# A two-layer trunk kernel on one core: T4 made in B21's buffer, and the two layer norms of the first ffn's end set beside other products

## The chip, the cores and the metric

The kernel runs on one core of one Trainium2 chip. Its time is device microseconds of one execution; the figure for a kernel is the median of several runs. The profile is of one further execution.

## The reference

Two streams of 256 tokens and width 1024, a context and a latent one, pass through two layers. Layer 0 mixes with a bidirectional mLSTM, layer 1 with latent attention (MLA), in which the latent queries see the keys and values of both streams. After each mixer comes a gated convolutional ffn, and after each sublayer a layer norm over the residual. Only the latent stream is returned. Cut to what matters here:

```
x = layer_norm(ALPHA * x + gate * mixer(h))           # both streams
f = (silu(dwconv(gate_part)) * up_part) @ ffn_w_out   # 2816 -> 1024
x = layer_norm(ALPHA * x + gate5 * f)                 # both streams
# layer 1, MLA: h = x * (1 + scale) + shift
kc, vc = kv(h_ctx)        # h @ w_dkv -> rms norm -> @ w_ukv
kl, vl = kv(h_lat)        # the same, with rotary keys
ql = rms_norm(h_lat @ w_dq) @ w_uq
y = attend(ql, [kc, kl], [vc, vl]) @ w_out
```

## The kernel before

Everything is float32. Each product runs as three float32r matmuls on halves "hi" and "lo" of both operands (`mm3`, L383 to L385): hi.hi, hi.lo, lo.hi. The halves are made by `split`: ScalarE copies (L388, for weights L323), VectorE subtracts (L389, L326).

**Weights** come through one stream in a fixed order (`_plan`). A tile of 128x1024 is loaded by the SP queue into a raw buffer (`_load`), split into one of three `w` buffers (or, when marked wide, into two buffers of the large pool `u`), used, and released. `use` splits ahead up to eight tiles, but no more than three `w` tiles live at once. The raw buffers form a ring; a tile takes the ring's next place.

**Value product and ffn output** (`w_v`, L787, and `w_fout0`, L1365) use a seven-product scheme of Strassen's kind over 2x2 blocks: four products on sums of weight blocks (vt2, v11, vt3, vt1; yt2, y11, yt3, yt1), then products with B21 (v21, y21), with T4 (vt4, yt4) and with B22 (v22, y22). T4 is T2 + B21 as the signs are set here: the sum T2 is formed by VectorE in the raw buffer (`_sum`, L292 to L294), written to DRAM as `t2d` when it is split (L325), and for T4 read back by SP (L278), after which POOL adds the block B21 from the weights with an adding load (L279). There are 14 such tiles, eight in `w_v` and six in `w_fout0`. In `w_v` the three last products alternate tile by tile; in `w_fout0` they run y21 (six tiles), y22 (six), yt4 (six, of which the last three by halves of the tokens).

**Around the ffn's end.** After the first four products of `w_fout0`, eight PSUM banks are held (p6, p1, p7, p5, two each). ScalarE copies p1 (u1, L1434), VectorE makes u2, u3, v and u4 from the others (L1437 to L1446). `residual` multiplies each by its gate (L1454) and adds ALPHA times the residual x1 (L1455), loaded by POOL from `x1d`. `add` (L1460) brings in the last products: gate, sum, statistics (L1464 to L1466). `z_norm` (L1502) normalises rows, `ln_T` (L1191) transposes them on TensorE and makes the modulated halves hc (context) and hl (latent) by L1206 to L1212; `ln_x` (L1217) writes the normed rows to DRAM for the next residual. Operands of y21, y22 and yt4 come back from DRAM and are converted (`operand`, L1386 and L1387).

**Order of the MLA part.** y22 ends the context's rows; the context's norm, its transposes and its dkv product come amid the yt4 tiles (`mid`, `mla_ctx`), then ukn(0), uv(0), uv(1) of the context run while the latent rows get their last product, norm and transposes in the background generator (`tick` takes one step of it); then in `mla` (L1633) the latent dkv and dq products, ukn(1), the query products and uv of the latent. Engine orders are the framework's scheduler's, except inside `manual_schedule`, where the program's order is kept, and for single pinned instructions. Limits on the stream (`st.limit`, PA, PB, PC with `pump`) time the splits of the wide tiles. `ffn_in` (L1292) of layer 1 runs its first pair of tiles with three matmuls per k and later pairs with two, one of them 512 columns wide (L1320), followed by a copy and an add.

Of the kernel before, what the change touches and what calls it, by code (L numbers as in the profile page):

```python
# [25 lines left out]
H1 = 8  # L26
# [11 lines left out]
PA, PB, PC = 0, 2, 4  # L38
# [18 lines left out]
YTAIL = 3  # L57
# [13 lines left out]
def _plan():  # L71
# [12 lines left out]
    for p in range(2):  # L84

        for j in range(4):
            for n in ("vt2", "v11", "vt3", "vt1"):
                add((n, p, j), 1024)
        for j in range(4):
            for n in ("v21", "vt4", "v22"):  # L90
                add((n, p, j), 1024)
# [15 lines left out]
    for n in ("y21", "y22", "yt4"):  # L107
        for j in range(6):
            if (n, j) == ("yt4", 6 - YTAIL):
                for c, m in enumerate((3, 3, 2)):  # L110
                    add(("dkv", 0, c), m * 320)
            add((n, 0, j), cols[j], n == "yt4" and j >= 6 - YTAIL)
# [4 lines left out]
    for c in range(4):  # L117
        add(("dq", 0, c), 768)
# [14 lines left out]
def _pack(i):  # L133
# [12 lines left out]
    for key, (n, cols) in ids.items():  # L146
        kind, a, c = key
        if kind == "up":
# [5 lines left out]
        elif kind[0] in "vy":  # L154

            x, y = {"11": (0, 0), "t1": (0, 1), "21": (1, 0), "t4": (1, 0)}.get(kind[1:], (1, 1))
# [78 lines left out]
class Stream:  # L235
# [26 lines left out]
    def _room(self):  # L262

        if self.nl >= self.n:
            return False
        j0, ring = self.ring(self.nl)
        tag = ring[(self.nl - j0) % len(ring)][0]
        return [self.tags[j] for j in self.raw].count(tag) < [x[0] for x in ring].count(tag)

    def _load(self):  # L270
# [3 lines left out]
        j0, ring = self.ring(j)  # L274
        tag, bufs = ring[(j - j0) % len(ring)]
        t = k.pool.tile([128, CW], F32, tag=tag, name="raw", bufs=bufs)
        if key[0] in ("vt4", "yt4"):
            k.nc.sync.dma_start(t[:, :cols], k.t2d[key[0][0], key[1], key[2]][:, :cols])  # L278
            k.nc.gpsimd.dma_start(t[:, :cols], self.ws[n, :, :cols], accum_op=ALU.add)  # L279
        elif key[0] not in ("vt2", "yt2"):  # L280
            k.nc.sync.dma_start(t[:, :cols], self.ws[n, :, :cols])
# [14 lines left out]
    def _split(self):  # L296
# [25 lines left out]
        else:  # L322
# [3 lines left out]
            k.nc.vector.tensor_sub(l[:, :cols], src, h[:, :cols])  # L326
        self.hl[j] = (h, l)
# [27 lines left out]
class K:  # L355
# [431 lines left out]
    def w_v(self):  # L787
# [16 lines left out]
        for p in range(2):  # L804
# [26 lines left out]
            p2, p4, p3 = pair("tok"), pair("tok"), pair("tok")  # L831
            for i in range(4):
                for name, ps, x in (("v21", p2, 2), ("vt4", p4, 3), ("v22", p3, "S4")):
                    w = st.use((name, p, i))
                    for h in range(2):
                        prod(ps, A[x, 2 * i + h], w, h, 2 * i + h)
                    self.tick(1)
                    if p == 1 and len(self.xc) < 16:
                        self.xc_load(len(self.xc) + len(self.xcr))
# [377 lines left out]
    def ln_x(self, ln, zs, dst):  # L1217
# [74 lines left out]
    def ffn_in(self, l, hT, n, nt, pre=(), both=None):  # L1292
# [6 lines left out]
        for p in range(NF):  # L1299
            pss = []  # L1300
            for j in range(2):
# [5 lines left out]
                else:  # L1307
# [13 lines left out]
                    if both is not None and p > 0:  # L1321
# [43 lines left out]
    def w_fout0(self, x1d, mid):  # L1365
# [4 lines left out]
        parts = [("2", i) for i in range(6)] + [("S4", i) for i in range(6)] + [("3", i) for i in range(6)]  # L1370
# [34 lines left out]
        n = 0  # L1405
        for i in range(6):
            for name, ps, x in (("yt2", p6, "S2"), ("y11", p1, "1"), ("yt3", p7, "S3"), ("yt1", p5, "S1")):
# [7 lines left out]
                if n >= 8:  # L1415
                    operand()
# [6 lines left out]
                if n >= 16 and n % 2 == 0:  # L1423
                    if n == 16:
                        z = []
                    t = self.uf("z")
                    nc.gpsimd.dma_start(t, x1d[len(z)])
                    z.append(t)
                n += 1
        stats = [self.tiny(12, "st").rearrange("p (a b) -> p a b", b=6) for _ in range(4)]  # L1430
        u1, u3, u4, vv = [], [], [], []
        for b in range(2):
            u = self.s2("u1")
            nc.scalar.copy(u, p1[b])  # L1434
            u1.append(u)
            u = self.s2("u2")
            nc.vector.tensor_tensor(u, p6[b], u1[b], op=ALU.add)  # L1437
            u4.append(u)
        for b in range(2):
            u = self.s2("u3")  # L1440
            nc.vector.tensor_tensor(u, p7[b], u4[b], op=ALU.add)
            u3.append(u)
        for b in range(2):
            v = self.s2("v")
            nc.vector.tensor_tensor(v, p5[b], u3[b], op=ALU.subtract)
            nc.vector.tensor_tensor(u4[b], p5[b], u4[b], op=ALU.subtract)  # L1446
            vv.append(v)

        def residual():

            for us, g, c in ((u1, 0, lo), (u4, 0, hi), (u3, 1, lo), (vv, 1, hi)):
                for b in range(2):
                    zz = z[2 * g + b]
                    nc.vector.tensor_tensor(us[b], us[b], gate[g][:, c], op=ALU.mult)  # L1454
                    nc.vector.scalar_tensor_tensor(zz[:, c], zz[:, c], ALPHA, us[b], op0=ALU.mult, op1=ALU.add)  # L1455
                    if us is vv:
                        nc.vector.bn_stats(stats[2 * g + b][:, 1], zz[:, c])
# [526 lines left out]
```

## Time and profile before

| what | value |
|---|---|
| median of 3 runs | 1385.51 us (1384.81 to 1386.47) |
| the profiled execution | 1386.22 us |
| its span in the trace | 1384.1 us |
| TensorE (PE) busy | 1354.0 us, 98% |
| VectorE (DVE) busy | 1090.0 us, 79% |
| ScalarE (ACT) busy | 713.1 us, 52% |
| DMA | 297.58 MB, mean 215 GB/s |

In the rows, PE is TensorE, DVE VectorE, ACT ScalarE, POOL GpSimd, SP the queue that loads weights. A row of the view in order of time reads: start, length, engine, source line, operation, output<-inputs, shape, count, and in brackets the idle time before it and what ended that. A row of the waits reads: engine and line that waited, engine and line that ended the wait, total us, times, longest. Matmul lengths overlap; the distance from start to start is what a matmul costs.

### The profile page before, as it was taken

Reading aid. Unit: us, or ns where it says so; the run is one execution under the profiler, and the core shown is the slowest. Engines: PE = TensorE matmul, PEld = TensorE weight load, DVE = VectorE, ACT = ScalarE, POOL = GpSimd, SP = SyncE. Lnnn points to the kernel's source line nnn. Section 1 sums busy time; section 2 is a strip of 40 time slices with the busy share of each in tenths; the row PEclk is TensorE's granted clock in tenths of the full one; section 3 lists DMA queues with packets and bytes.
Section 4 is the critical chain, followed back from the end, with each engine's and each line's share of the span. In section 5 each row is a group of like instructions: output and inputs, shape, how many; then the busy total and the mean of one; then the engine's idle time right before and its main releaser. Section 6 shows DMA issues by size and latency. Waiting matters only on the chain.

```text
span 1384.1 us, 18592 instructions
## 1 busy us (share of the span) xinstructions
PE 1354.0 (98%) x6567; PEld 1123.2 (81%) x6567; DVE 1090.0 (79%) x1768; ACT 713.1 (52%) x1221; POOL 121.6 (9%) x215
## 2 busy tenths in 40 slices
PE   7999999999999999999999999999999999999997
PEld 3788888888788888878898888888777888888886
DVE  6598857687688697779799878668898789788873
ACT  6585534435444555364643434334637567466660
POOL 0033000011011011120002000000001001000100
PEclk9999999999999999999999999999999999999999
DMA  9689847789666364766747877646987425256750
GB/s 338 227 293 316 290 156 247 239 286 302 214 200 204 105 232 132 250 193 228 241 147 239 300 230 234 212 145 229 312 231 226 137 99 202 109 185 185 252 202 31
DMA packets 97900, 297.58 MB, mean 215 GB/s; under 512 B 12136, under 2 KB 24808, under 8 KB 97808
## 3 DMA queue, kind: packets, MB, share of 16 engines
q1 hardware_dynamic: 68672, 218.52, 47.5%
q0 software_dynamic: 17472, 57.57, 13.3%
q10 hardware_dynamic: 11664, 20.32, 4.1%
q8 instruction: 51, 0.84, 0.2%
q14 instruction: 41, 0.34, 0.1%
HBM read 262.90 MB, written 33.46 MB: 214 GB/s over the span
## 4 chain that ended last, share of the span: by engine, by line
PE 91%; DVE 5%; ACT 2%; issue 1%; DMA 0%; SPq 0%; DVEq 0%; ACTq 0%
PE fin L1320 9%; PE fin L383 6%; PE fin L384 6%; PE fin L385 6%; PE tok L383 6%; PE tok L384 6%; PE tok L385 6%; PE y L384 5%; PE y L385 5%; PE y L383 5%; PE qk L383 4%; PE qk L385 4%; PE qk L384 4%; PE up L383 2%; PE up L385 2%; PE up L384 2%
## 5 line engine op out<-in xcount | busy, mean ns | idle before, releaser
L326 DVE TENSOR_TENSOR w<-raw,w 128x1024 fp32r<-128x1024 f32 (+3 forms) x290 | 348.1, 1203 | 141.3 <-ACT w L323 140.3
L323 ACT CAST w<-raw 128x1024 fp32r<-128x1024 f32 (+3 forms) x290 | 300.4, 1037 | 306.2 <-PE tok L385 88.6
L512 DVE SCALAR_TENSOR_TENSOR junk<-ar,bc 128x1024 f32<-128x1024 f32 x128 | 156.0, 1218 | 4.9 <-ACT bc L554 2.1
L384 PE MATMUL fin<-h,w 128*128 128x512 f32 (+1 forms) x376 | 141.2, 376 | 0.0
L385 PE MATMUL fin<-h,w 128*128 128x512 f32 (+1 forms) x376 | 140.9, 375 | 0.0
L383 PE MATMUL fin<-h,w 128*128 128x512 f32 (+1 forms) x376 | 140.8, 376 | 0.1
L1320 PE MATMUL fin<-h,w 128*128 128x256 f32 (+1 forms) x640 | 113.0, 339 | 0.0
L1320 PEld LDWEIGHTS fin<-h,w 128*128 128x128 f32 x640 | 98.2, 189 | 14.7
L383 PE MATMUL qk<-xc,w 128*128 128x512 f32 x256 | 100.7, 393 | 0.0
L385 PE MATMUL qk<-xc,w 128*128 128x512 f32 x256 | 99.9, 390 | 0.0
L384 PE MATMUL qk<-xc,w 128*128 128x512 f32 x256 | 99.8, 390 | 0.0
L384 PEld LDWEIGHTS fin<-h,w 128*128 128x128 f32 x376 | 70.8, 188 | 12.9 <-DVE h L1212 0.2
L385 PEld LDWEIGHTS fin<-h,w 128*128 128x128 f32 x376 | 70.8, 188 | 12.9
L383 PEld LDWEIGHTS fin<-h,w 128*128 128x128 f32 x376 | 70.5, 188 | 13.1 <-ACT h L1211 0.3
L383 PEld LDWEIGHTS qk<-xc,w 128*128 128x128 f32 x256 | 48.1, 188 | 10.0 <-issue 0.4
L385 PEld LDWEIGHTS qk<-xc,w 128*128 128x128 f32 x256 | 48.1, 188 | 9.9
L384 PEld LDWEIGHTS qk<-xc,w 128*128 128x128 f32 x256 | 48.1, 188 | 9.7
L383 PE MATMUL up<-hT,w 128*128 128x512 f32 x128 | 50.5, 394 | 0.5 <-ACT hT L388 0.5
L384 PE MATMUL up<-hT,w 128*128 128x512 f32 x128 | 50.1, 392 | 0.5 <-DVE hT L389 0.5
L385 PE MATMUL up<-hT,w 128*128 128x512 f32 x128 | 50.1, 391 | 0.3 <-DVE w L389 0.3
L383 PE MATMUL tok<-w,hT 128*128 128x512 f32 x128 | 49.8, 389 | 0.0
L384 PE MATMUL tok<-w,hT 128*128 128x512 f32 x128 | 49.8, 389 | 0.0
(463 smaller groups left out, 3151.2 us busy)
## 6 DMA issues: line engine op xcount, KB each, us to landing
raw<-in_ws SPq DMA_DIRECT2D x287, 512.0 KB, 4.3
ar<-in_adaT SPq DMA_DIRECT2D x80, 512.0 KB, 4.6
adaw<-in_ada_w SPq DMA_DIRECT2D x32, 256.0 KB, 6.7
t2d<-raw ACTq DMA_DIRECT2D x13, 512.0 KB, 4.9
raw<-t2d SPq DMA_DIRECT2D x13, 512.0 KB, 6.3
raw<-in_ws POOLq DMA_DIRECT2D x13, 512.0 KB, 8.0
zr<-fd ACTq DMA_DIRECT2D x33, 128.0 KB, 3.9
xmd<-xr POOLq DMA_DIRECT2D x16, 256.0 KB, 5.0
```

The source lines that it names most:

```text
L323: k.nc.scalar.copy(h[:, :cols], src)
L326: k.nc.vector.tensor_sub(l[:, :cols], src, h[:, :cols])
L383: mm(out, w[0], x[0], start=start, stop=False)
L384: mm(out, w[0], x[1], start=False, stop=False)
L385: mm(out, w[1], x[0], start=False, stop=stop)
L512: nc.vector.scalar_tensor_tensor(o, w, 1.0, self.bc[j], op0=ALU.mult, op1=ALU.mult, accum_out=col[:, k, j:j + 1])
L1320: nc.tensor.matmul(o, a, b, start=k == 0 and i == 0, stop=k == 7 and i == 1)
```

## The change

T4 is no longer loaded. When v21 or y21 has been split, POOL adds `t2d` into the raw buffer that still holds B21, and that buffer is T4's raw tile; a buffer is therefore held longer, and `_load` takes any free place of the ring in place of the next one. The orders of the products follow two written lists, V_ORDER and Y_ORDER. In `w_fout0` y21 and yt4 now alternate with PE and DVE in program order, and y22 comes last. u1 is copied as soon as p1 is complete. The residual is added by POOL's adding loads of `x1d`, which `ln_x` of layer 0 writes already multiplied by ALPHA. yt4's end completes the latent rows: their norm and transposes run in the background beside y22 (PE in program order). The context's rows are completed by y22: their norm is emitted before the latent dkv, their transposes after the latent dq. In `mla` the latent keys and values come first, then the context's dkv, and the rest. The pumps go; dkv tiles are wide.

```
+V_ORDER = [("v21", 0), ("v22", 0), ("v21", 1), ("v22", 1), ("vt4", 0), ("v21", 2), ("v22", 2), ("vt4", 1),
+           ("v21", 3), ("v22", 3), ("vt4", 2), ("vt4", 3)]
+Y_ORDER = [("y21", 0), ("y21", 1), ("y21", 2), ("y21", 3), ("yt4", 0), ("y21", 4), ("yt4", 1), ("y21", 5),
+           ("yt4", 2), ("yt4", 3), ("yt4", 4), ("yt4", 5)]
...
 in _plan, after the first four products of the ffn output
+    for n, j in Y_ORDER:
+        add((n, 0, j), cols[j])
+    for j in range(6):
+        add(("y22", 0, j), cols[j])
+    for c, m in enumerate((3, 3, 2)):
+        add(("dkv", 0, c), m * 320, True)
+    for c in range(4):
+        add(("dq", 0, c), 768)
...
 in _load
-            k.nc.sync.dma_start(t[:, :cols], k.t2d[key[0][0], key[1], key[2]][:, :cols])
-            k.nc.gpsimd.dma_start(t[:, :cols], self.ws[n, :, :cols], accum_op=ALU.add)
...
 in _split, after the subtraction
+        if key[0] in ("v21", "y21"):
+            i = [x[0] for x in self.order].index((key[0][0] + "t4",) + key[1:])
+            k.nc.gpsimd.dma_start(src, k.t2d[key[0][0], key[1], key[2]][:, :cols], accum_op=ALU.add)
+            self.raw[i], self.tags[i] = raw, self.tags[j]
...
 in ln_x, scale = ALPHA for layer 0's first norm
-                nc.vector.tensor_tensor(zs[t][:, c], zs[t][:, c], g[h], op=ALU.mult)
-                nc.vector.tensor_tensor(zs[t][:, c], zs[t][:, c], b[h], op=ALU.add)
+                nc.vector.scalar_tensor_tensor(zs[t][:, c], zs[t][:, c], scale, g[h], op0=ALU.mult, op1=ALU.mult)
+                nc.vector.scalar_tensor_tensor(zs[t][:, c], b[h], scale, zs[t][:, c], op0=ALU.mult, op1=ALU.add)
...
 in ffn_in
-                        if both is None or p == 0:
+                        if both is None or p < 2:
...
 in w_fout0
-                if n >= 8:
+                if n >= 6:
                     operand()
...
+                if (name, i) == ("y11", 5):
+                    for b in range(2):
+                        u = self.s2("u1")
+                        pin(nc.scalar.copy(u, p1[b]))
+                        u1.append(u)
...
+        z = [self.uf("z") for _ in range(4)]
+        def sums():
+            def part(us, g, c):
                 for b in range(2):
+                    zz = z[2 * g + b][:, c]
+                    nc.vector.tensor_tensor(zz, us[b], gate[g][:, c], op=ALU.mult)
+                    nc.gpsimd.dma_start(zz, x1d[2 * g + b][:, c], accum_op=ALU.add)
...
+        with self.tc.manual_schedule(engines={e.PE, e.DVE}):
+            self.bg.append(sums())
+            for n, (name, i) in enumerate(Y_ORDER):
+                ps, x = pr[name]
+                if not ps:
+                    ps += pair()
+                w = st.use((name, 0, i))
+                prod(ps, x, w, i)
+                if n == 8:
+                    self.drain()
+                    self.bg.append(add(0, lo, pr["y21"][0]))
+                self.tick(1)
+                operand()
+                if n == 11:
+                    for b in range(2):
+                        nc.vector.bn_stats(stats[2 + b][:, 1], z[2 + b][:, hi])
         self.drain()
+        self.bg = [add(1, lo, pr["yt4"][0]), self.z_norm(z[2:4], stats[2:4]), latent(z[2:4])]
+        with self.tc.manual_schedule(engines={e.PE}):
+            ps = pair()
+            for i in range(6):
+                w = st.use(("y22", 0, i))
+                prod(ps, "S4", w, i)
+                self.tick(2)
+            self.drain()
+        for _ in add(0, hi, ps):
+            pass
+        for _ in self.z_norm(z[0:2], stats[0:2]):
+            pass
+        return z[0:2]
...
 in ukn, per pair of heads
+            if h % 2:
+                for i in range(2):
+                    u = self.kn[h - 1 + i]
+                    self.split(u[:, 0, cs], u[:, 1, cs], ps[:, i * 256:(i + 1) * 256])
...
 mla(hl, hc, ctx): the order of its products
+        self.rope_load()
...
+        wd = [st.use(("dkv", 0, c)) for c in range(3)]
+        rows2 = self.dkv_rows(self.dkv_mm(hl, wd), 2)
         pss = [self.ps("dq0"), self.ps("dq1")]
...
+        self.dkv_T(rows2, 2)
+        ctx()
+        rows = self.dkv_rows(self.dkv_mm(hc, wd), 0)
+        self.take_late()
+        self.tick()
...
+        self.ukn(1)
+        self.tick()
+        self.uv((2, 3))
+        self.dkv_T(rows, 0)
         cq = []
...
+        self.ukn(0)
+        self.tick()
...
+        self.uv((0, 1))
...
 in build
+        def latent(zs):
+            cols = k.ln_mod_cols(1, 1, 0, 0)
+            hlu.extend([k.u("hl") for _ in range(4)])
+            yield from k.ln_T(zs, *cols, hl, True)
+            k.late.append(k.ln_x(1, zs, [x2d[0], x2d[1]]))
+        def ctx():
+            hcu.extend([k.u("hc") for _ in range(4)])
+            for _ in k.ln_T(zc, *k.ln_mod_cols(1, 1, 0, 1), hc, False):
+                pass
+        st.limit = [x[0] for x in order].index(("aout", 0, 0))
+        zc = k.w_fout0(x1d, latent)
+        att = k.mla(hl, hc, ctx)
```

More of the change, by code (lines that the diff above doesn't have):

```diff
@@ L88, in _plan @@
                 add((n, p, j), 1024)
-        for j in range(4):
-            for n in ("v21", "vt4", "v22"):
-                add((n, p, j), 1024)
+        for n, j in V_ORDER:
+            add((n, p, j), 1024)
     add(("gates", 0, 0), 256)
@@ L1439, in w_fout0 @@
[L1439 to L1451, printed above, removed]
-                for b in range(2):
[L1453 to L1457, printed above, removed]
-                    yield
+                n += 1
```

210 lines of the change are left out of this document (73 added, 137 removed).

## The prediction

> **What bounds the kernel now.** I read the page, then what TensorE waited for in the stretch that the change rewrites, then that stretch by windows, then each engine's rows there in order of time. First the page and the windows (columns: us, busy time and instruction count of each engine, granted clock, DMA share, GB/s; the last three rows are of a query for PE alone).
>
> ```profile
> span 1384.1 us, 18592 instructions
> ...
> PE 1354.0 (98%) x6567; PEld 1123.2 (81%) x6567; DVE 1090.0 (79%) x1768; ACT 713.1 (52%) x1221; POOL 121.6 (9%) x215
> ```
> ```profile
> 190.00:360.00 170.00, 170.00 (x751) 140.45 (x750) 127.79 (x141) 78.18 (x94) 14.81 (x22) 1.00 0.78 249
> ...
> 1000.00:1045.00 45.00, 40.68 (x176) 31.91 (x175) 44.77 (x70) 21.98 (x29) 6.96 (x9) 1.00 0.84 234
> ```
> ```profile
> 1076.00:1080.00 4.00, 2.40 (x14) 0.94 0.00 0
> 1080.00:1084.00 4.00, 4.00 (x20) 0.64 0.00 0
> 1000.00:1100.00 100.00, 91.89 (x479) 0.98 0.70 212
> ```
>
> PE bounds the whole: 30.1 us of 1384.1 are idle. The value product (190 to 360) has no idle PE at all, so reordering it can only lose. The change can win in 1000 to 1100, where PE idles 100 - 91.89 = 8.1 us; and in 1000 to 1045 DVE is busy 44.77 of 45 us, so there DVE is the bound. Who ended PE's waits in 1000 to 1100:
>
> ```profile
> PE y L384 <- DVE w L326: 2.1, 2, 1.4
> PE y L383 <- ACT u L1434: 1.5, 1, 1.5
> PE dkv L383 <- ACT hl L1211: 1.5, 1, 1.5
> PE v L384 <- DVE wu L326: 0.8, 2, 0.5
> PE kn L383 <- ACT ckT L1576: 0.7, 1, 0.7
> PE zT L1199 <- DVE z L1513: 0.5, 1, 0.5
> PE dkv L383 <- ACT hc L1211: 0.3, 1, 0.3
> PE kn L385 <- DVE wu L326: 0.3, 1, 0.3
> ```
>
> The eight add up to 7.7 of the 8.1 us. One more loss is no wait: behind the wait on hl the same 320-column product is slower for a while.
>
> ```profile
> 1078.41 0.42 PE L383 MATMUL dkv<-w,hl 128*128 128x320 f32 x1 [1.51 <-ACT hl L1211]
> ...
> 1080.49 0.47 PE L385 MATMUL dkv<-w,hl 128*128 128x320 f32 x1
> 1080.76 0.47 PE L383 MATMUL dkv<-w,hl 128*128 128x320 f32 x1
> ...
> 1084.08 0.31 PE L384 MATMUL dkv<-w,hl 128*128 128x320 f32 x1
> 1084.22 0.31 PE L385 MATMUL dkv<-w,hl 128*128 128x320 f32 x1
> ```
>
> Starts are 0.27 us apart at a granted clock of 0.64 and 0.14 later. By the windows this cost 4 x (1 - 0.64) + 4 x (1 - 0.94) = 1.7 us. So 8.1 + 1.7 = 9.8 us can go at most; everything else in the sum is set against that.
>
> [...]
>
> **The change, part by part.** PE's rows set the unit: one weight tile of these products is twelve matmuls, here the first of one tile and the first of the next.
>
> ```profile
> 986.61 0.39 PE L383 MATMUL y<-w,fa 128*128 128x512 f32 x1
> ...
> 989.33 0.39 PE L383 MATMUL y<-w,fa 128*128 128x512 f32 x1
> ```
>
> A step is 2.72 us; the last tile (i = 5) is half, 1.36 us. DVE's costs, from instructions back to back:
>
> ```profile
> 1014.19 0.68 DVE L1455 SCALAR_TENSOR_TENSOR z<-z,u 128x512 f32<-128x512 f32 x1
> 1014.79 0.68 DVE L326 TENSOR_TENSOR w<-raw,w 128x512 fp32r<-128x512 f32 x1
> 1015.39 0.68 DVE L1454 TENSOR_TENSOR u<-u,gate 128x512 f32<-128x512 f32 x1
> ...
> 1016.93 1.22 DVE L326 TENSOR_TENSOR w<-raw,w 128x1024 fp32r<-128x1024 f32 x1
> 1018.07 0.68 DVE L1454 TENSOR_TENSOR u<-u,gate 128x512 f32<-128x512 f32 x1
> ```
>
> 512 columns take 0.60 us from start to start, 1024 take 1.14, by width 768 take 0.87, 960 1.07 and 640 0.73.
>
> *T4 by an adding load.* Out go 14 SP loads of t2d and 14 POOL loads of the weights, in come 14 POOL loads of t2d into B21's buffer: 14 transfers fewer, and PE waited for none of them. The price is a chain: B21's split, POOL's issue, landing, T4's split. Rows for it:
>
> ```profile
> 998.78 1.23 DVE L326 TENSOR_TENSOR w<-raw,w 128x1024 fp32r<-128x1024 f32 x1 [0.53 <-ACT w L323]
> ```
> ```profile
> 999.17 1.05 ACT L323 CAST w<-raw 128x1024 fp32r<-128x1024 f32 x1
> ```
> ```profile
> L279 POOL DMA_DIRECT2D raw<-in_ws x14: 866/882/1053, 226.7 to 1041.1; - x14
> ...
> DMA to landing us min/median/max: 5.4/8.2/10.1
> ```
>
> With three w buffers a tile's split starts when PE leaves the third tile before it. At v21,3 and vt4,3, three places apart in V_ORDER, B21's split needs 1.05 + 1.23, the load 8.2, T4's split again 2.28: 12.8 us, against five PE steps, 13.6. Spare 0.8 us at the median; at the longest landing 1.1 late, at the shortest 3.6 spare. For yt4,0: y21,0's split ends at 1000.0, landing 1008.2, T4 ready 1010.5; PE, its first y21 product at 1000.2, wants it four steps later at 1011.1. Spare 0.6; worst 1.3 late. The other eleven stand four to six places apart and have over 2 us to spare by the same count. Three tight places (two in the value product) cost 0 to 3.5 us together; I take 0.3 each, 0.9, near the median landing, with something for DVE's lag. While ACT and DVE wait for a late load, in order, the next tile's split, sums and (on POOL) the next adding load are queued behind; two tiles are ready ahead, 5.4 us.
>
> *Residual by adding loads.* Eight DVE multiply-adds (L1455, 4.8 us) become eight POOL adding loads of 256 KB, and four POOL loads of x1d go; each has some three steps or more before its reader. The factor ALPHA moves into ln_x as a two-operation form: the first rows above show that form at the same 0.60 us, so nothing. Operands start two steps earlier (four conversions leave the crowded stretch).
>
> *u1 copied early, PE and DVE order fixed.* L1434's wait (1.5) goes, since p1 is complete 2.72 us before the phase ends and ACT copies it there; I leave 0.2. The DVE waits (2.1): count DVE's work for the eleven steps of y21/yt4 and the 5.5 of y22, 16.5 x 2.72 = 44.9 us. Splits 13 x 1.14 + 3 x 0.60 = 16.6; dkv tiles 2 x 1.07 + 0.73 = 2.9; two dq tiles 1.7; 16 sums and gates 9.6; two adds, 12 x 0.60 = 7.2; two statistics and two operands 2.4; z_norm's two rows 1.5 by the chain below; the latent's transposed rows 12 x 0.38 = 4.6 (an L1212 pair takes 0.76). Sum 46.5 us: 104% of PE's time, where before 44.77 stood beside 40.68. Two tiles of lead carry the 1.6 us; I leave 1.0 (0 to 2.1).
>
> ```profile
> 1046.76 0.76 DVE L1212 TENSOR_TENSOR hc<-zm,hc 128x256 fp32r<-128x256 f32 x2 [1.09 <-ACT hc L1211]
> ```
>
> *The latent's norm beside y22.* In before the same chain runs for the context behind y22:
>
> ```profile
> 1036.28 1.28 DVE L1464 TENSOR_TENSOR zp<-y,gate 128x512 f32<-128x512 f32 x2
> ...
> 1044.13 0.54 DVE L1513 TENSOR_SCALAR z<-z,mv,rs 128x512 f32<-128x512 f32 x1
> ```
> ```profile
> 1044.71 0.81 ACT L1514 ACTIVATE z<-z,nm,rs 128x512 f32<-128x512 f32 x1
> ```
>
> From 1036.28 to 1045.52 is 9.2 us. After, the ticks put the first transposes behind the fourth y22 tile, 4 x 2.72 = 10.9 us after yt4's end. Cover 1.7 us, less DVE's lag: I leave 0.5. The hl wait (1.5) and its dip (1.7) go, as hl's last columns have the fifth and sixth tiles and the first dkv products above them. If the cover is gone, the price is the lag itself plus a dip of 1.7.
>
> *The context's norm beside the latent dkv and dq.* Same 9.2 us under 48 products of dkv, 0.145 each, 7.0 us, and 48 of dq, 384 columns wide and so between 0.145 and 0.227, some 8 us. Its transposes must still be evacuated before the context's dkv: the 0.5 and 0.3 of before become 0.4. The ukn and uv tiles are split during dq, well ahead, so the wu waits (0.8 + 0.3) go. ckT then kn remains the same chain, now for the context: 0.7 stays, as do the 0.4 us that no wait names. Rope's two SP loads move behind the dkv tiles' loads with 15 us before the transposes need their rows: nothing. Splitting kn by pairs and dropping pumps and ticks: no instruction more or less, nothing.
>
> *fin1, second pair.* Two matmuls per k become three of 256 columns:
>
> ```profile
> 1195.00 0.28 PE L384 MATMUL fin<-h,wu 128*128 128x256 f32 x1
> 1195.12 0.28 PE L385 MATMUL fin<-h,wu 128*128 128x256 f32 x1
> ```
> ```profile
> 1196.85 118.42 PE fin L1320 x672
> ```
>
> 16 x (3 x 0.12 - 2 x 118.42 / 672) = +0.1 us. The copy and add that go were off PE's path.
>
> **Sum.** Left or new: 0.9 + 0.2 + 1.0 + 0.5 + 0.4 + 0.7 + 0.4 + 0.1 = 4.2. Gain 9.8 - 4.2 = 5.6. The profiled execution took 1386.22 (its span and 2.1 outside), so 1380.6; it lay 0.71 above the median of the runs, 1385.51, so in those terms **1379.9 us**, 0.4% faster.
>
> **Rivals.** (a) *The stalls only move.* DVE's 46.5 us against 44.9 bunch where dkv's splits meet the latent norm. With two or three splits more ahead of L1513 than in before, PE idles 2.9 us there in place of 0.5, and the clock dips as it did behind hl: 2.4 + 1.7 back, 1384.0. For it: DVE full at 104%. Against it: the eight multiply-adds are gone and DVE's order is fixed.
>
> (b) *The adding loads land late; slower.* The place is the three tight chains: every us of a landing beyond 8.9 (8.2 and the spare 0.7) stops PE at each, and a stop of 1.5 us or more can cost 1.7 of clock too (it did behind one of the two waits of 1.5). Up to 10.4 us the three cost 3 x 1.5 = 4.5 and the change still gains; from there the clock joins in, 3 x 3.2 less the 0.9 counted, 1388.6, and at 12.2 us 3 x (3.3 + 1.7) less 0.9, 1394.0. For it: the longest seen is 10.1. Against it: with DVE full the six issues in 1018 to 1041 landed no later:
>
> ```profile
> DMA to landing us min/median/max: 5.4/7.7/9.9
> ```
>
> [...]
>
> (c) *All of it goes*, tight chains included: 9.8 less 0.1 and the 0.4 that no wait names, 9.3, 1376.2.
>
> **How the numbers follow.** What a measurement here can tell from no change is about 0.2%, 2.8 us: 1382.7 to 1388.3. Forecast 0.55, (c) 0.08, (a) 0.23, (b) 0.14. So faster 0.63, same 0.23, slower 0.14. The range goes from (c), 1376.2, to 1386.5: the forecast with its unknowns at their worst (3.5 for the loads, 2.1 for DVE: 1383.6) and (a) with a second split's delay (2.5 more). Left out is (b) and a little on either side.
>
> **What would show it.** Right: PE idle in the stretch from y21 to cqT falls from 8.1 to about 3.5; no granted clock under 0.9 at the latent dkv; no wait on u1, hl or wu; the value product without idle PE. Wrong: PE waiting on DVE's split of vt4 or yt4 with the adding load as what ACT waited for; a wait of zT on L1513 inside y22; a new clock dip at the context's dkv; DVE idle for ACT inside y21/yt4.

## The result and the profile after

The changed kernel takes 1392.51 us (median of 4 runs, 1392.2 to 1393.79), the kernel before beside it 1385.99 (4 runs, 1384.81 to 1386.8). The ratio is 1.0051 with a 95% interval of 1.0036 to 1.0066: 0.5% slower, where 0.4% faster was forecast. The profiled execution after took 1392.22 us, 6.0 more than the one before; its span is 6.3 longer.

First the page of the changed kernel, its lines for the span and for the engines' busy time:

```profile
span 1390.4 us, 18564 instructions
...
PE 1354.4 (97%) x6583; PEld 1125.8 (81%) x6583; DVE 1084.7 (78%) x1758; ACT 712.2 (51%) x1219; POOL 126.3 (9%) x219
```

PE works as long as before (1354.0), so nothing was added to its work: it stands still longer. The windows of the changed kernel, all engines (us, then busy time and count of PE, PEld, DVE, ACT, POOL, then granted clock, DMA share, GB/s):

```profile
190.00:360.00 170.00, 170.00 (x750) 140.51 (x749) 127.07 (x142) 78.05 (x94) 14.58 (x22) 1.00 0.73 225
1000.00:1045.00 45.00, 40.27 (x165) 31.37 (x164) 37.37 (x49) 20.85 (x26) 12.37 (x14) 0.96 0.96 233
```

The value product still has no idle PE. The second row is the surprise: DVE, forecast to be full at 104%, is busy 37.37 of 45 us, where it was 44.77. It does less, and PE still waits for it. The waits of PE from 995 to 1112, and windows for PE alone:

```profile
PE y L400 <- DVE w L337: 3.2, 4, 1.5
PE ckT L1596 <- DVE ckr L1584: 2.9, 1, 2.9
PE zT L1216 <- DVE z L1538: 2.7, 2, 1.6
PE y L399 <- ACT w L334: 1.5, 1, 1.5
PE ckT L1596 <- DVE ckr L1549: 0.7, 1, 0.7
PE kn L399 <- ACT ckT L1600: 0.4, 1, 0.4
```
```profile
1000.00:1010.00 10.00, 7.71 (x26) 0.83 0.94 272
...
1050.00:1054.00 4.00, 1.29 (x6) 0.88 0.89 249
1054.00:1058.00 4.00, 4.00 (x17) 0.69 0.85 340
...
1078.00:1082.00 4.00, 1.75 (x9) 0.79 1.03 388
1082.00:1086.00 4.00, 4.00 (x26) 0.78 0.36 142
...
1000.00:1110.00 110.00, 98.51 (x517) 0.95 0.67 187
```

The waits on u1, on hl and on the wide tiles (wu) are gone, as forecast. In their place stand four others. Idle time from 1000 to 1110 is 110 - 98.51 = 11.5 us, the waits add up to 11.4. The clock fell three times, by 10 x 0.17, by 4 x (0.12 + 0.31) and by 4 x (0.21 + 0.22): 1.7 us each, 5.1 in all. Together 16.6, against 9.8 before. These 6.8 us stand beside the 6.3 by which the span grew: the loss lies in this stretch, and the small rest outside it.

**Where the four waits come from** is read from the queues behind them, row by row. ScalarE, then VectorE, of the changed kernel:

```profile
1000.35 0.62 ACT L1403 CAST fz<-zr 128x512 fp32r<-128x512 f32 x1 [2.14 <-DMA raw<-in_ws]
1000.88 1.06 ACT L1445 COPY u<-y 128x512 f32<-128x512 f32 x2
...
1001.83 1.05 ACT L334 CAST w<-raw 128x1024 fp32r<-128x1024 f32 x1
...
1027.00 0.99 ACT L334 CAST wu<-raw 128x960 fp32r<-128x960 f32 x1 [3.68 <-DMA raw<-in_ws]
1027.90 1.99 ACT L334 CAST w<-raw 128x1024 fp32r<-128x1024 f32 x2
1033.38 1.58 ACT L334 CAST w<-raw 128x512 fp32r<-128x512 f32 x2 [3.49 <-DMA raw<-t2d]
...
1072.50 0.36 ACT L1546 ACTIVATE ckr<-dkv 128x256 f32<-128x256 f32 x1
...
1072.86 1.04 ACT L334 CAST wu<-raw 128x1024 fp32r<-128x1024 f32 x1
...
1073.99 1.55 ACT L334 CAST w<-raw 128x1024 fp32r<-128x1024 f32 x2
1077.79 1.04 ACT L334 CAST w<-raw 128x1024 fp32r<-128x1024 f32 x1 [2.24 <-DVE ckr L1559]
1078.74 0.38 ACT L1546 ACTIVATE ckr<-dkv 128x256 f32<-128x256 f32 x1
```
```profile
1028.97 1.23 DVE L337 TENSOR_TENSOR w<-raw,w 128x1024 fp32r<-128x1024 f32 x1 [3.20 <-ACT w L334]
```

- *First y21 product* (2.3 us and a dip). The split of y21's first tile is the row at 1001.83. Ahead of it stand u1's copies, and ahead of those an operand (the row at 1000.35) for which ScalarE stood still 2.14 us, until a *weight* load had landed.
- *T4's tiles and the first y22 tile* (2.45 us: 0.94 at two T4 tiles, 1.51 at y22's first). At 1027.00 ScalarE has waited 3.68 us for the raw data of a dkv tile (960 columns, wide), which PE first uses at 1060.67. Behind it, in order, stand the splits of two T4 tiles; VectorE sat idle 3.20 us for the first. Next comes a wait of 3.49 on T4's last adding load, and the row at 1033.38 has that half tile and, behind it, the first of y22.
- *Transposes of the normed latent rows* (2.7 and a dip): weight splits stand between the statistics and the scaling, on both engines.
- *Transposes of the latent kv rows* (3.65 and a dip). The latent dkv product ends at 1067.9. The rms norm of its second row tile starts at 1078.74: between the two ScalarE has split six weight tiles, five of them for products behind the transposes.

All four have one form: an instruction on the chain stands, in an in-order queue, behind a weight split or an operand's conversion that is needed later or whose data is late on the chip. That the scheduler puts it there because it reckons it ready is argued, not shown.

### The profile page after: what moved, and what is told of

It reads as the page before. It is cut to its first block, busy times and chain, and to the rows that moved or that the text cites. A ratio compares the mean times of both kernels' runs of the same rounds, so it can differ in the third digit from the quotient of the medians.

```text
span 1390.4 us, 18564 instructions
## 1 busy us (share of the span) xinstructions
PE 1354.4 (97%) x6583; PEld 1125.8 (81%) x6583; DVE 1084.7 (78%) x1758; ACT 712.2 (51%) x1219; POOL 126.3 (9%) x219
## 4 chain that ended last, share of the span: by engine, by line
PE 88%; DVE 5%; DMA 4%; ACT 2%; issue 1%; SPq 0%; DVEq 0%; ACTq 0%
PE fin L1337 8%; PE fin L399 6%; PE fin L400 6%; PE fin L401 6%; PE tok L399 6%; PE tok L400 6%; PE tok L401 6%; PE y L400 5%; PE y L401 5%; PE y L399 5%; PE qk L399 4%; PE qk L401 4%; PE qk L400 4%; DMA raw<-in_ws 2%; PE up L399 2%; PE up L401 2%
## 5 line engine op out<-in xcount | busy, mean ns | idle before, releaser
L337 DVE TENSOR_TENSOR w<-raw,w 128x1024 fp32r<-128x1024 f32 (+1 forms) x290 | 348.1, 1203 | 150.4 <-ACT w L334 144.2
L334 ACT CAST w<-raw 128x1024 fp32r<-128x1024 f32 (+1 forms) x290 | 299.9, 1036 | 302.4 <-PE tok L401 90.8
```

The source lines that it names most:

```text
L334: k.nc.scalar.copy(h[:, :cols], src)
```

## The experiments

The order theory: the places of the splits in the queues of ScalarE and VectorE cost the time. Its main rival, the load theory: the adding loads land late. Medians below stand beside 1386.1 to 1386.5 for the kernel before in the same series (15 to 28 runs); ratios are to it. Single executions of one kernel lie up to 7.5 us apart (rms_first: 1387.78 to 1392.96, the profiled one the lowest), so waits are read from the profile, times from the medians.

**One place at a time.**

```
pin_dkv, in _split:
-            k.nc.scalar.copy(h[:, :cols], src)
+            (k.tc.keep_in_program_order if key[0] == 'dkv' else id)(k.nc.scalar.copy(h[:, :cols], src))
norm_first, in z_norm, on each of its six instructions:
+            with self.tc.high_priority(300): ...
rms_first, in dkv_rows:
+            with self.tc.high_priority(300): self.rms(ps[:, 0:256], 256, r[:, 0:256])
```

> The changed kernel with one addition: ScalarE's copy of each dkv tile is pinned behind the splits traced before it, so the first one no longer stands ahead of the splits of the T4 tiles. Order theory (the splits of dkv tiles, whose raw data lands late, stand ahead of T4's splits in ScalarE's queue and hold them and VectorE up): PE's wait on T4's weights (3.2 us in the profile after) falls to 1 us or less, the wait of zT on the normed rows (2.7 us) shrinks with it and the clock dip behind it may go; 2 to 5 us less than the changed kernel's 1392.5, so 1387.5 to 1390.5. Load theory (the adding loads themselves land too late): ScalarE then waits for T4's raw tile in place of dkv's, PE's wait stays at 3 us, 1391.5 to 1393.

> The changed kernel with the norm of the rows (statistics, reciprocal, the two scalings) at a higher priority for the scheduler, so that fewer weight splits stand between the statistics and the scaled rows. Order theory: the wait of zT (2.7 us and its clock dip of 1.7) shrinks by the one or two splits of 0.7 to 1.2 us that are passed: 1 to 4 us less, 1388.5 to 1391.5. Load theory: the rows are late because the tiles before them were; nothing changes by more than 0.5 us, 1392 to 1393.

> The changed kernel with the rms norm of the dkv rows at a higher priority for the scheduler, so that it passes the splits of the query weights on ScalarE and VectorE. Order theory: the transposes behind the latent dq no longer wait (0.7 + 2.9 us, and the clock dip of 1.7 there): 3 to 5 us less, 1387.5 to 1389.5. The rival for this place is that the product order alone sets it (the rows end too short a time before the transposes): then 1 us or less is gained, 1391.5 or more.

Measured: 1390.06 (ratio 1.0025, 1.0016 to 1.0033), 1389.16 (1.0020, 1.0011 to 1.0028) and 1390.52 (1.0029, 1.0018 to 1.0041; 1 us over what was expected). Each takes back 2 to 3.4 of the 6.5 us. ScalarE with dkv's copies pinned, then PE's waits with the kv rows' norm first:

```profile
1032.93 2.52 ACT L334 CAST w<-raw 128x512 fp32r<-128x512 f32 x3 [4.90 <-DMA raw<-t2d]
```
```profile
PE zT L1216 <- DVE z L1538: 2.7, 2, 1.6
PE zT L1216 <- ACT zm L1223: 2.2, 1, 2.2
...
PE ckT L1596 <- DVE ckr L1584: 0.6, 1, 0.6
```

With dkv's copies out of the way, ScalarE waits at the same place for T4's last adding load, 4.90 us: both theories hold there, one late load stood behind the other, and PE's stop shrinks only from 2.45 to 1.75. In the same profile the wait ahead of the latent kv rows grew to 4.6 us, so the idle time is that of the changed kernel; what went is one dip of the three. Its trace does not show where the 2.45 us by which the median fell come from. With the norm first, the wait of zT falls from 2.7 to 1.1 and its dip goes, as the order theory has it. With the rms first, ckT waits 0.6 in place of 3.65, but the context's transposes behind it now wait 2.2.

**Which load is at fault.**

```
t4y_loaded: yt4 alone as in the kernel before
+        if key[0] == "yt4": k.nc.sync.dma_start(t[:, :cols], k.t2d["y", ...]); k.nc.gpsimd.dma_start(t[:, :cols], self.ws[...], accum_op=ALU.add)
x1_loaded, ahead of the last products:
+                    for t in range(4):
+                        nc.gpsimd.dma_start(z[t], x1d[t])
...
 in part():
-                    nc.vector.tensor_tensor(zz, us[b], gate[g][:, c], op=ALU.mult)
-                    nc.gpsimd.dma_start(zz, x1d[2 * g + b][:, c], accum_op=ALU.add)
+                    nc.vector.tensor_tensor(us[b], us[b], gate[g][:, c], op=ALU.mult)
+                    nc.vector.tensor_tensor(zz, zz, us[b], op=ALU.add)
```

> The changed kernel with T4 of the ffn output alone loaded as in the kernel before (SP brings the sum back, POOL adds the weights from DRAM in a buffer of its own); the value product keeps the new form. Load theory: PE's wait on T4's weights (3.2 us) goes and the rest behind it comes earlier, 1387 to 1390. Order theory: what is late is the place of dkv's tiles in the queues and the held raw places; since six more tiles need raw places, the loads of dkv and dq come later still and something of 2 us either way follows; with dkv's first split left ahead of T4's the wait stays, 1391 to 1394.

> The changed kernel with the residual loaded whole by POOL ahead of the last products and added by VectorE (eight additions more, 4.8 us), in place of eight adding loads. Load theory: the last adding load of T4, issued among six adding loads within 4 us, lands 11.9 us after its issue; with only T4's own left it lands after some 7, the waits at 1030 to 1040 (2.5 us) go, 1389 to 1391. Order theory: the wait there is dkv's split ahead of T4's, and VectorE has 4.8 us more to do in a stretch in which it is full: 1393 to 1396.

Measured: 1392.62 (1.0051, 1.0037 to 1.0066), no change; and 1397.46 (1.0080, 1.0066 to 1.0094), 5.0 slower, a little over the order theory's range. In the first the time is the same and the stops are not. T4's stops go, as the load theory has it, but the one at the first y21 product grows from 2.3 to 5.5 us, behind an operand that ScalarE could not convert before a weight load had landed:

```profile
1003.51 0.62 ACT L1403 CAST fz<-zr 128x512 fp32r<-128x512 f32 x1 [5.20 <-DMA raw<-in_ws]
```

Six adding loads of T4 in the ffn output, in the changed kernel and then with the residual loaded plain:

```profile
DMA to landing us min/median/max: 5.7/9.7/11.9
```
```profile
DMA to landing us min/median/max: 3.9/6.6/7.9
```

So the residual's adding loads do make T4's land later, by 3.1 us at the median. But taking them away gives VectorE eight additions back (8 x 0.6 = 4.8 us), and the kernel loses about that. The residual's part of the change is worth its 5 us.

**The start of the last products.**

```
operands_n8:                                    t4_later, with operands_n8:
-                if n >= 6:                     Y_ORDER: y21 0 1 2 3 4, yt4 0, y21 5, yt4 1 2 3 4 5
+                if n >= 8:
```

> The changed kernel with the operands of the last three products started at the ninth step as in the kernel before, not at the seventh; u1 is still copied early. Order theory: the first y21 product is late since ScalarE waits 2.1 us at an operand's load that shares a semaphore with a weight load, with u1's copies and y21's first split queued behind; with the operands later, another load stands there and the split comes earlier: the 2.3 us of idle time and 1.7 of clock at 1003 fall to under 1, so 1388.5 to 1391. Rival (the weights' load itself is late, or four operand conversions more in the crowded stretch cost as much): 1391.5 to 1394.

> Two edits: operands from the ninth step, and the first T4 tile one place later (y21's tiles 0 to 4, then yt4's tile 0, y21's tile 5 and the other T4 tiles). Load theory for the start of the stretch: with operands from the ninth step alone PE stopped for 3.2 us at the first T4 tile, whose adding load landed 7.6 us after its issue; one place later, 2.7 us, that stop falls to 0.5 or less and its clock dip goes: 1386.5 to 1389. If the stop comes from the place of the operands in VectorE's queue instead, it stays: 1390 to 1392.

Measured: 1390.44 (1.0028, 1.0017 to 1.0039) and 1387.76 (1.0013, 1.0004 to 1.0022). PE and ScalarE with the operands from the ninth step:

```profile
1001.52 0.50 PE L400 MATMUL y<-w,fz 128*128 128x512 f32 x1 [0.30 <-DVE w L337]
1013.30 0.80 PE L400 MATMUL y<-w,fz 128*128 128x512 f32 x1 [3.19 <-DVE w L337]
```
```profile
1009.76 1.05 ACT L334 CAST w<-raw 128x1024 fp32r<-128x1024 f32 x1 [3.30 <-DMA raw<-t2d]
...
1010.76 0.62 ACT L1403 CAST fz<-zr 128x512 fp32r<-128x512 f32 x1
```
```profile
1011.41 0.69 DVE L1404 TENSOR_TENSOR fz<-zr,fz 128x512 fp32r<-128x512 f32 x1 [3.45 <-ACT fz L1403]
1012.02 1.22 DVE L337 TENSOR_TENSOR w<-raw,w 128x1024 fp32r<-128x1024 f32 x1
```

The first stop is gone (0.3 us), and near the tight place of rival (b) another comes out from under it. By the count of matmuls, twelve to a tile, the product that stops 3.19 us at 1013.30 is not T4's: it is y21's fourth tile, one place ahead. The first T4 tile's adding load lands at 1009.7; ScalarE has waited 3.30 us for it, an operand's conversion stands behind, and VectorE, idle 3.45 us, comes to y21's fourth tile only at 1012.02. A late load and an in-order queue make this stop together. With T4 one place later in the order it is 0.6. It was hidden only because y21 was late itself. The wait at y22's first tile, 1.51 us in the changed kernel, is 3.03 here; the median gains 2.1 us.

**The limit on the stream.**

```
limit_back: st.limit at ("ukn", 0, 0); behind self.dkv_T(rows2, 2): st.pump(aout)
uv_limit:   st.limit at ("uv", 0, 0); behind the context's dkv product: st.pump(aout)
```

> The changed kernel with a limit on the stream in place of the pumps that went: the four wide tiles of ukn and uv and what follows them are split only behind the transposes of the latent kv rows. Order theory: four splits of 1.0 us on ScalarE and 1.1 us on VectorE leave the place between the end of the latent dkv product and the rms norm of its rows, so the transposes wait for 1 us or less in place of 3.6 and the clock dip of 1.7 us there goes: 3 to 5 us less, 1387.5 to 1389.5, more of it than what the higher priority alone brought. Rival (the order of the products leaves too little time for the rows): 1391 or more. Should the split tiles come late for the ukn product instead, a wait of kn on VectorE's wu stands in the profile.

> The changed kernel with the limit on the stream set at the uv tiles and lifted behind the context's dkv product, where TensorE is busy for 7 us and nothing else is split; ukn's two tiles stay where they are. Order theory: two wide splits and the query tiles behind them (some 5.8 us on VectorE) leave the place ahead of the latent kv rows and come where they collide with nothing, so the transposes' wait (3.6 us and 1.7 of clock) falls to about 1 us and no wait on hc comes in its place: 3 to 5 us less than the changed kernel, 1387.5 to 1389.5. Rival (VectorE has no room anywhere in this part): as with the limit at ukn, a wait on hc in its place, 1391 to 1396.

Measured: 1395.95 (1.0067, 1.0055 to 1.0080), slower, on the rival's side; and 1390.04 (1.0031, 1.0018 to 1.0043), 0.5 us above what was expected. PE's wait with the limit at ukn, then at uv:

```profile
PE dkv L399 <- ACT hc L1228: 5.1, 1, 5.1
```
```profile
PE zT L1216 <- DVE ckT L1601: 1.4, 1, 1.4
```

Both take the splits from ahead of the latent kv rows, and the 3.65 us there go. With ukn's tiles among them, the splits come just where the context's transposes are evacuated, and the context's dkv product waits 5.1 us for hc. Held until that product runs, the two uv tiles collide with less: 1.4 us on zT in place of the 3.65, and the median falls by 2.5. The place decides; the work is the same.

**Edits together.** four_undone is pin_dkv, norm_first, operands_n8 and limit_back; all_together is pin_dkv, norm_first, t4_later (with operands_n8) and uv_limit.

> Four edits of order together, no work added or removed: dkv's copies pinned behind the splits traced before them, the row norm at a higher priority, the operands started at the ninth step, the limit on the wide ukn and uv tiles. Order theory: the four places (first y21 product, T4's weights, transposes of the normed rows, transposes of the kv rows) hold 11.1 us of idle time and 5.1 of clock in the profile after; if two thirds go the kernel takes 1382 to 1385, faster than both. Rival (what is removed at one place comes back at the next, since VectorE is full): 1387 or more.

> Five edits of order, no work added or removed: operands from the ninth step, the first T4 tile one place later, dkv's copies pinned behind the splits traced before them, the row norm at a higher priority, the limit at the uv tiles. Order theory: of the 11.5 us of idle time and 5.1 of clock in the stretch some 4 and 1.7 are left, so 1380 to 1384, faster than both kernels. Rival (the stalls only move, VectorE and ScalarE being full): 1386 or more.

Measured: 1389.86 (1.0026, 1.0017 to 1.0036), and **1382.20 (0.9970, 0.9960 to 0.9979)**, faster than both kernels: 0.3% under the one before, 10.3 us under the changed one. The first lies on the rival's side: it still has the 5.1 us on hc and a 2.7 us stop at y21's fourth tile. The second, PE's waits and its window:

```profile
PE zT L1216 <- DVE ckT L1601: 2.7, 1, 2.7
PE y L400 <- DVE w L337: 2.6, 4, 1.2
PE zT L1216 <- DVE z L1538: 1.1, 1, 1.1
PE kn L399 <- ACT ckT L1600: 0.4, 1, 0.4
```
```profile
1000.00:1110.00 110.00, 103.15 (x552) 0.98 0.68 194
```

Idle time is 6.85 us where the changed kernel had 11.5, more than the 4 that were expected, and one dip is left of three.

> The five edits of order together, and the transposes of the latent kv rows moved behind the context's dkv product. In the five edits' profile the context's transposes waited 2.7 us behind them (for VectorE at the latent kv halves). Order theory: that wait goes, a wait on hc and one ahead of the kn product come back for some 1.5 us together, so 0 to 2 us less than 1382.2: 1380.2 to 1382.2. Rival (the rows' chain takes the same time wherever it stands): the kn product waits as long, 1382 to 1385.

```
all_kvT_later: self.dkv_T(rows2, 2) moved from ahead of ctx() to behind the context's dkv product
```

Measured: 1384.86 (0.9991, 0.9981 to 1.0001), in the rival's range at its upper end. The wait of zT goes and the context's dkv product waits 2.4 us for VectorE.

**What T4 in B21's buffer is worth by itself.**

```
value_t4_alone: the kernel before, with V_ORDER and the adding load for v21/vt4 only
all_t4_loaded:  all_together, with vt4 and yt4 loaded as in the kernel before
```

> The kernel before with one part of the change alone: T4 of the value product made in B21's buffer, with the new order of its last products; nothing of the ffn output or the mla part. Both theories: no idle time of PE in the value product, the same time as before within 0.2%, 1384 to 1388. A cost of the adding loads by themselves (14 transfers fewer, POOL's issues the same) would show here as over 1388.5.

> The five edits of order together, with all 14 T4 tiles loaded as in the kernel before (SP brings the sum back, POOL adds the weights from DRAM in a buffer of their own); the orders of the products are those of the changed kernel. Theory that T4 in B21's buffer gains nothing by itself: the loads were hidden, so the time stays at 1381 to 1384. Rival (the 14 transfers fewer free SP's queue and the raw places in the full stretch): 1386 or more. If the adding loads cost by landing late in the tight places: under 1380.5.

Measured: 1388.58 (1.0020, 1.0011 to 1.0029) and 1392.06 (1.0044, 1.0031 to 1.0056). The first lies just over the expected range, the second on the rival's side. In the full set of edits T4's new form is worth 9.9 us; without those edits it had changed nothing for yt4 (t4y_loaded, 1392.62 against 1392.51). With all T4 tiles loaded, PE stops longest at y21's fifth tile, not at T4, behind an operand whose own load ScalarE waited 4.65 us for. That kernel's PE and ScalarE, and the landing of its adding loads from 985 to 1045:

```profile
1022.99 0.79 PE L400 MATMUL y<-w,fz 128*128 128x512 f32 x1 [4.50 <-DVE w L337]
```
```profile
1020.46 0.62 ACT L1403 CAST fz<-zr 128x512 fp32r<-128x512 f32 x1 [4.65 <-DMA zr<-fd]
```
```profile
DMA to landing us min/median/max: 5.5/12.4/15.1
```

And the value product's T4 alone, which leaves the value product without idle PE, costs 2.2 us, 640 us later. ScalarE and PE of that kernel:

```profile
988.29 5.39 ACTq L1397 DMA_DIRECT2D zr<-fd  x2
993.78 0.62 ACT L1403 CAST fz<-zr 128x512 fp32r<-128x512 f32 x1 [4.44 <-DMA raw<-in_ws]
...
1004.35 0.62 ACT L1403 CAST fz<-zr 128x512 fp32r<-128x512 f32 x1 [3.25 <-DMA raw<-in_ws]
```
```profile
1007.73 0.79 PE L399 MATMUL y<-w,fz 128*128 128x512 f32 x1 [5.75 <-ACT u L1451]
```

u1's wait, 1.53 us before, is 5.75. In the traces of the kernel before and of the changed one the transfers of SP's and ScalarE's queues signal their landing on the same eight semaphores, in turn (before: 460 of SP and 81 of ScalarE, 67 or 68 on each), POOL's 208 on eight others. There a load goes out only when the one that had its semaphore before has landed: on the three semaphores whose landings both traces hold in full (104, 106, 107) none of 395 went out earlier, the closest 0.02 us after. In the changed kernel the operand's load ahead of the row at 1000.35 went out at 999.92, when the weight load that SP had issued at 996.11 on the same semaphore landed (999.90). With the value product's T4 alone, the row at 988.29 has 5.39 us for two issues of an operand's loads, and the conversion behind it waited 4.44 us until a weight load had landed, with all of ScalarE's later work behind. Two things can have changed. Eight loads fewer on SP's queue shift the turns: the 3.25 us at the later operand end with a weight load's landing, where in the kernel before its load (at 998.06) follows another operand's (992.33) on its semaphore, and ScalarE does not wait. And the weight loads themselves may land later: in the kernel before the first of these operands follows a weight load too, issued at 984.43 and landed at 988.19, but there the two issues took 1.72 us, not 5.39, and ScalarE waited 0.76 us, not 4.44. To test the first, the operands were loaded by POOL, whose transfers in those traces share no semaphore with SP's:

```
-                    pin(nc.scalar.dma_start(r[:, h * 256:(h + 1) * 256], ...))
+                    pin(nc.gpsimd.dma_start(r[:, h * 256:(h + 1) * 256], ...))
```

> The kernel before with T4 of the value product alone made in B21's buffer, and the operands of the ffn output's last products loaded by POOL, whose loads share no semaphore with SP's weight loads, in place of ScalarE's queue. Without the second edit PE stopped for 5.8 us at 1002, behind a ScalarE whose operand loads waited 4.4 and 3.3 us for weight loads. Shared-semaphore theory: ScalarE no longer waits for weight loads at the operands, the stop falls to 1.5 us or less as in the kernel before, and the time to 1383 to 1386. Late-weights theory (the weight loads themselves are late, since the raw places are taken in another order): the stop stays at 3 us or more, 1387.5 or more.

> The kernel before with the operands of the ffn output's last products loaded by POOL in place of ScalarE's queue: the control for the run beside it. Shared-semaphore theory: the stop of 1.5 us at the first last product stays or shrinks, as ScalarE waits 0.5 us there for an operand: 1384 to 1386.5. Late-weights theory: the same, 1385 to 1387.

> The changed kernel with the operands loaded by POOL. Shared-semaphore theory: ScalarE's wait of 2.1 us ahead of the first y21 split goes and with it the 2.3 us of idle time and 1.7 of clock at 1003; the first T4 tile, ready 8 us behind the first y21 split, may then stop PE for some 3 us, as it did with operands from the ninth step: 1388 to 1391. Late-weights theory: nothing changes there, 1391.5 to 1394.

> The five edits of order together, and the operands loaded by POOL. Shared-semaphore theory: what is left of waits on operand loads goes too, 0 to 2 us less than the five edits alone (1382.2), 1380 to 1382.2. Rival (POOL's queue then holds up T4's adding loads, with 0.9 us for each issue): the first T4 tile is late again, 1383 to 1386.

Measured, in this order: 1387.98 (1.0012, 1.0003 to 1.0021), 1385.86 (0.9999, 0.9990 to 1.0008), 1390.01 (1.0028, 1.0016 to 1.0039), 1385.46 (0.9995, 0.9986 to 1.0003). PE in the first and in the third:

```profile
1004.27 0.50 PE L399 MATMUL y<-w,fz 128*128 128x512 f32 x1 [2.66 <-ACT u L1451]
```
```profile
1011.24 0.50 PE L400 MATMUL y<-w,fz 128*128 128x512 f32 x1 [1.01 <-DVE w L337]
```

In the changed kernel the stop at the first y21 product goes altogether, and y21's fourth tile is 1.0 us late, behind an operand: the operand's wait for a weight load was the first stop's cause. With the value product's T4 alone the stop halves, from 5.75 to 2.66 against 1.84 in the control, but the time falls only 0.6 us, since waits of 3.4 us on VectorE's weights follow. Its 1387.98 is not the 1383 to 1386 of the shared-semaphore theory, it lies in the range of the late-weights theory, and it is still 2.1 us over its control: taking the shared semaphores away gave back 0.6 of those 2.2 us at most, and the rest is open. The last run lies on the rival's side: POOL's queue then holds T4's adding loads and the operands together, ScalarE waits up to 5.09 us for an operand, and 3.3 us are lost.

## Why the prediction was wrong

Its terms for what is left or new, beside the changed kernel's profile (in us; idle time, and clock where it fell):

| term | forecast | measured |
|---|---|---|
| adding loads, value product | 0.6 | 0 |
| adding load of the first yt4 tile | 0.3 | 0, since y21 was late; 3.2, at y21's fourth tile, once it was not |
| start of the last products (u1) | 0.2 | 2.3 + 1.7 |
| DVE's weights | 1.0 | 2.45, 1.51 of it at y22 |
| latent norm's chain | 0.5 | 2.7 + 1.7 |
| context's chain | 0.4 | 0 |
| dropped pumps and ticks, order of the mla part | 0 | 3.65 + 1.7 |
| ckT then kn | 0.7 | 0.4 |
| no wait names it | 0.4 | 0 |

With 0.1 forecast for fin1 the middle column is 4.2, the right one 16.6.

- **Right:** the value product without idle PE; the waits on u1, hl and wu gone; the context's chain covered; the residual's adding loads, whose eight multiply-adds were priced at 4.8 us and cost 5.0 when VectorE got eight additions back; and the sentence that behind a late load the next tile's split is queued. That came one place ahead of rival (b)'s, at y21's fourth tile, in two kernels where y21 itself was no longer late: 3.2 us and, one place later in the order, 0.6.
- **The step that failed first:** "Splitting kn by pairs and dropping pumps and ticks: no instruction more or less, nothing." True of the count, false of the order. Without the pumps the splits of ukn, uv and the query tiles stood ahead of the latent kv rows. The prediction had itself put those splits "during dq, well ahead", and counted only the waits on wu that this removes. It was the largest term, 5.35 us. A limit at the right place took its 3.65 us of wait away and brought 1.4 elsewhere.
- **The second:** VectorE's sum. 46.5 us of work against 44.9 was set against two tiles of lead, as if the queue ran whenever there was work. VectorE was in fact busy less than before and idle 45 - 37.37 = 7.6 us, waiting for ScalarE's copies, which waited for loads. Rival (a) named the right mechanism, with splits ahead of L1513's counterpart and a dip behind, and priced 4.1 us for one place; the profile has 4.4 there (2.7 + 1.7). That the same thing would happen at three more places was in no rival.
- **The third:** "Operands start two steps earlier", counted only as work taken out of the crowded stretch, and 0.2 left for the start of the last products, which measured 4.0. The earlier operands met weight loads still under way (2.14 us at 1000.35), and u1's copies and y21's first split stood behind them. With the operands at their old place the stop is 0.3 us, with their loads in POOL's queue it is gone.
- **The fourth:** "14 transfers fewer, and PE waited for none of them", so no cost. The eight of the value product alone, with the new order, cost 2.2 us on the kernel before, in a stretch that this part does not touch. Freeing the operands from the weight loads gave 0.6 us of it back; the cause of the rest is not shown.
- **Rope:** its two loads, priced at nothing, waited 10.2 us in SP's queue for T4's raw places, the second until 1030.22, and held the weight loads behind them. No run separates what that cost; it stays open, as does the rest of the first stop in value_t4_alone (2.66 against 1.84).

The clock: the dip that the prediction counted with the wait on hl stands behind 1.51 us of idle time, PE's longest gap from 1060 to 1086 in the kernel before. The three dips of the changed kernel stand behind idle gaps of 1.52 and 0.77, of 1.59 and 1.12, and of 2.95 us.

## What to carry to other kernels

Count an edit's effect on the *order* of each in-order queue, not only its instructions: a limit, a pump or a load that goes is free in work and can still let a split that waits for data slip ahead of the chain. When a full engine's forecast is off, look first at whether it was full: an idle engine that PE waits for points one queue further back. A change whose parts are worth something in one order (5.0 us for the residual in the changed kernel, 9.9 for T4 in the mended one) can measure slower as a whole, so put its order right before giving it up. What a part is worth hangs on that order: T4 in the value product alone cost 2.2 us. And no run gives the kernel before such edits of order, so how much of the final 0.3% is the change, and how much a better order that the old kernel could have had too, is open.

## What the runs showed of the hardware

A dip of the clock cost 1.7 us three times in the changed kernel, behind gaps of different length. In its trace the granted clock is 0.50 in three stretches of 3.4 us, 1005.26 to 1008.67, 1053.05 to 1056.46 and 1080.35 to 1083.77, and 3.4 x 0.5 = 1.7; the kernel before has one such stretch there, 1079.48 to 1082.90. It is not the price of every dip. With the operands from the ninth step, behind the stop of 3.19 us, the mean granted clock was 0.57 over eight us, 8 x 0.43 = 3.4 us:

```profile
1012.00:1020.00 8.00, 6.70 (x18) 0.57 0.94 191
```

When it falls is not settled by the gap: with the limit at uv the gaps at the first y21 product were 2.17 and 0.77 us, against 1.52 and 0.77 in the changed kernel, and the clock stayed full:

```profile
1000.00:1010.00 10.00, 7.07 (x30) 1.00 0.89 272
```

T4's adding loads in the ffn output landed between 3.9 and 11.9 us after their issue, earlier without the residual's eight beside them (median 6.6 against 9.7); with the weights added from DRAM they took up to 15.1, at a median of 12.4.
